# A hybrid attention trunk on one core: the next head's keys are turned two blocks earlier, the old head's end one block later

## The chip, the core and the metric

The kernel runs on one core of a Trainium2 chip. Its engines each work through an instruction stream of their own and meet at semaphores: TensorE (PE in the profile, with its weight loads as PEld), VectorE (DVE), ScalarE (ACT, called Activation below), GpSimd (POOL) and SyncE (SP), which issues most of the transfers. The metric is the device time of one execution in microseconds, lower is better. A comparison is between medians of several runs on the same chip.

## What is computed

One layer of a diffusion trunk over 512 latent tokens and 128 context tokens, width 1024, all in float32: a gated feed-forward half-step, a token mixer, a second half-step. The change lies in the mixer's differential attention, 8 heads, each with two query/key pairs of width 64 and a value of width 128:

```python
dq = rmsnorm(dq.reshape(B, T, DA_HEADS, 2, DA_HEAD_DIM), p['g_qn'][l])
dk = rmsnorm(dk.reshape(B, T, DA_HEADS, 2, DA_HEAD_DIM), p['g_kn'][l])
q_att = rope_2d(dq)                                   # latent tokens
keys = jnp.concatenate([rope_2d(dk), k_ctx], axis=1)  # 512 own, 256 cached
s = jnp.einsum('bqhcd,bkhcd->bhcqk', qi, kf) * scale
pr = jax.nn.softmax(s, axis=-1)
w = pr[:, :, 0] - lam * pr[:, :, 1]
att = jnp.einsum('bhqk,bkhv->bqhv', w, vf)
att = rmsnorm(att, p['g_sub'][l]) * (1.0 - lam_init)
```

Beside it the same input projection feeds an mLSTM branch, whose gate rows also pass through this stage of the kernel.

## The kernel before, in words

Products are made float32-accurate by splitting an operand into a high part (rounded by Activation) and the rest (a subtraction on VectorE), so that one product is three matmuls (`mm3`).

**The attention stage** is a loop over 8 heads (L2091) and, in each, over 5 blocks of 128 queries (`qi` 0 to 3 latent, 4 context). A block is: `scores` (8 matmuls into one PSUM tile, of which there is one), a minimum over it on VectorE (`mn`, L1716), `soft` (two exponentials on Activation, tiles `p`), `mix` (reciprocals and one combination on VectorE), `turn` (the mixed weights are transposed on TensorE, `ps_wT`, and copied out by Activation, `wT`; in blocks 0 to 3 six transposes, in block 4 one) and `values` (matmuls into `ps_o`, scaled into `ao` by VectorE). The steps are pipelined: `turn` and `values` of one block stand in the next.

Between these steps stand **fill units**, slices of the remaining projections (`fill.units`), which keep TensorE occupied. From head 1 on most of them are wide: 12 matmuls of 512 columns into the single tile of the pool `ps2w`, which Activation empties in two copies (`k_tok`/`q_tok`, later `v_tok`/`stage`). Other PSUM tiles of this stage rotate through four buffers (tag `mm`).

**A head's beginning.** The queries and keys lie token by token. `turned` (L1656) transposes them on TensorE (`ps_qkT`), Activation copies them to the tile `qk_t`, and four transfers lay them out as `qk_d`. `queries` then makes `qT` (one Activation copy, one VectorE subtraction), and `keys` makes `kH` and `kL` from the cached keys `ck` and from `qk_d`. Before, queries are turned in block 3 of the head ahead and keys in block 4; `queries` and `keys` stand behind that head's last block.

**A head's end.** `finish_norm` (L1757) normalises `ao` on Activation and VectorE. `finish` (L1766, kept as `late` until the next head) transposes the result (`ps_aT`), copies it to `aT` and sends that to `aT_dram`.

**One buffer for four tiles.** The tag `asq` has a single buffer, shared by `qk_t`, the square in `finish_norm`, `aT`, and in heads 2 and 4 the gate rows `QQ`, which `gate_load` (L1505) fetches at the end of block 1 and `gate_cols` (L1508) transposes on TensorE in block 2 (`ps_c`):

```python
Q_at[0] = j, load(ap, [128, T], qq_dram[:, j, :], tag="asq", name="QQ")
```

So each of these users waits until the one before has left the buffer; for `aT` that is when its transfer to `aT_dram` has landed.

**What sets the order.** TensorE's instructions keep the program's order (`mm` and `tr` call `keep_in_program_order`). Activation and VectorE instructions inside `with written():` keep the written order among themselves on their engine; the rest, and the transfers without a fixed order, are placed by the framework's scheduler when the kernel is built. On each engine and on SP's queue what comes out is a fixed sequence: an instruction that waits holds up all behind it.

**Rotations.** `rotate` (L1581) does one step at a time of the norm and rope of the next pair of heads' queries and keys, in place, on Activation and VectorE. Keys and queries of a pair of heads must be through before they are turned; in both versions they are.

Of the kernel before, what the change touches and what calls it, by code (L numbers as in the profile page):

```python
# [31 lines left out]
def tile_trunk(ctx: ExitStack, tc: tile.TileContext, a: dict):  # L32
# [35 lines left out]
    @contextmanager  # L68
    def written():
        was, as_written[0] = as_written[0], in_row  # L70
        yield
        as_written[0] = was
# [1336 lines left out]
    fill = Fill()  # L1409
# [171 lines left out]
    def rotate():  # L1581

        if not rotations:
            return False
        first, second = rotations[0], rotations[1] if len(rotations) > 1 else []
        had, left = len(first), len(second)
        with written():
            if had == 4 and left == 7 or had == 2 and left == 5:
                second.pop(0)()
            else:  # L1590
                first.pop(0)()
                if (had, left) in ((5, 8), (4, 6)):
                    second.pop(0)()
            if not first:
                rotations.pop(0)
        return True
# [190 lines left out]
    def begin_pools():  # L1787
        gates.close()
        late_p.append(late_of.enter_context(tc.tile_pool(name="late", bufs=1, reuse_waits="tile")))
        fill.spare = late_p[0]  # L1790
# [3 lines left out]
    def begin_memory():  # L1794
        assert not rotations and not any(isinstance(g[0], tuple) for g in fill.q)
        fill.spare = None
        late_of.close()
        in_pools["k"] = ctx.enter_context(tc.tile_pool(name="mlk", bufs=1, side="right", reuse_waits="tile"))
        load_keys(0)
        load_queries(0)  # L1800
# [171 lines left out]
    heads = [Head(hd) for hd in range(8)]  # L1972
# [81 lines left out]
    rope_p[0] = ap  # L2054
    gt = gates.enter_context(tc.tile_pool(name="gates", bufs=1))
    heads[0].load_cache()
    heads[0].turn_queries()
    heads[0].turn_keys()
    fill.units(3)
    heads[0].queries()  # L2060
    heads[0].keys(0, 1, 2)
    fill.units(4)
# [7 lines left out]
    def aside(hd, qi, part):  # L2070
        if hd == 0:
            for _ in range(ROWS.get((qi, part), 0)):
                next(rows, None)
        if part == 0:
            with written():
                split = fill.low()
            if qi < 4 and (UNITS[hd][qi][1] or not split):
                rotate()
        elif qi != 3:
            rotate()  # L2080
        if (qi, part) == (1, 1) and hd in (2, 4):
            gate_load(hd // 2 - 1)
        if (qi, part) == (2, 0) and hd in (2, 4):
            gate_cols()
# [5 lines left out]
    late = None  # L2090
    for hd in range(8):  # L2091
        H = heads[hd]
        odd = hd % 2
        N = heads[hd + 1] if hd < 7 else None
        for qi in range(5):
            n = UNITS[hd][qi]
            with written():
                H.scores(qi)
                if qi > 0:
                    H.turn(qi - 1)  # L2100
                H.soft(qi)
            aside(hd, qi, 0)
            fill.units(n[0])
            with written():
                H.mix(qi)
            if late is not None:
                late()
                late = None
            if qi > 0:
                with written():  # L2110
                    H.values(qi - 1)
            if qi == 3 and hd < 7:
                while odd and rotate():
                    pass
                with written():
                    N.turn_queries()
                N.load_cache()
            if qi == 4 and hd < 7:
                with written():
                    N.turn_keys()  # L2120
            aside(hd, qi, 1)
            if (hd, qi) == (0, 2):
                begin_pools()
            elif (hd, qi) == (6, 2):
                begin_memory()
            fill.units(n[1])
            if n[1]:
                rotate()
            with written():
                fill.ahead()  # L2130
        n = UNITS[hd][-1]
        with written():
            H.turn(4)
        if hd < 7:
            with written():
                N.queries()
                N.keys(0)
            fill.units(n[0])
            with written():
                H.values(4)  # L2140
                N.keys(1, 2)
            H.finish_norm()
            fill.units(n[1])
            with written():
                fill.ahead()
            fill.units(n[2])
            late = H.finish
        else:
            fill.eager = True
            fill.units(1)  # L2150
            H.values(4)
            H.finish_norm()
            fill.drain(3)
            with written():
                H.finish()
# [514 lines left out]
def build(nc, shapes):  # L2670
    a = {}
    for n, s in shapes.items():
        a[n] = nc.dram_tensor("in_" + n, s, F32, kind="ExternalInput").ap()
    for n, s in _OUTS.items():
        a[n] = nc.dram_tensor("out_" + n, s, F32, kind="ExternalOutput").ap()
    with tile.TileContext(nc, schedule_with_timeline_sim=True) as tc:
        tile_trunk(tc, a)
# [21 lines left out]
```

## Time and profile before

| | us |
|---|---|
| median of 3 runs | 1819.51 (1816.02 to 1820.16) |
| the profiled execution | 1823.29 |
| its span, first to last instruction | 1821.5 |
| TensorE busy | 1776.0 (98 % of the span) |
| VectorE busy | 1340.9 (74 %) |
| Activation busy | 892.9 (49 %) |
| mean granted TensorE clock | 0.995 |

The stage of the change runs from about 655 to 1095 us of the span. In the answers shown below, a row of the timeline has the start, the busy time, engine, line, operation and tiles (out<-in), how many instructions are merged in it, and in brackets the idle time ahead of it on its engine with what ended that. Rows of an engine's waits give the total, the number and the longest. `SPq` marks SP's queue, on which the time is that of issuing a transfer; the time to its landing is told apart.

### The profile page before, as it was taken

The page shows a single profiled execution, that of the slowest core. Times are in us where ns is not written, and L with a number is a line of the kernel's source. Part 1 is how long each engine was busy: PE and PEld are TensorE (multiplying, and loading weights), DVE is VectorE, ACT ScalarE, POOL GpSimd, SP SyncE. Part 2 cuts the span into 40 slices and gives each one's busy share as a digit, 9 for nine tenths or more (in the row PEclk, how much of TensorE's full clock was granted, in tenths as well). Part 3 has the DMA queues.
Part 4 walks back from the last instruction along what each step waited for, and adds up shares of the span by engine and source line. Part 5 has one row for each costly group of instructions (what it writes and reads, how often), then busy time and mean ns, then how long its engine had stood idle before and what let it go on. Part 6 is the DMA issues. An engine that isn't in the chain of part 4 may idle for free.

```text
span 1821.5 us, 29435 instructions
## 1 busy us (share of the span) xinstructions
PE 1776.0 (98%) x11790; PEld 1706.8 (94%) x11790; DVE 1340.9 (74%) x2136; ACT 892.9 (49%) x1563; POOL 40.8 (2%) x72
## 2 busy tenths in 40 slices
PE   8999999989999999999999999999999999999998
PEld 6999999989999999877878998889999999999998
DVE  5979987667888848667675546877677888997485
ACT  4554544332655455555654536563326545454432
POOL 0000000100000000000000000000000000000010
PEclk9999999999999999999999999999999999999999
DMA  8355566968235553333334336566652445557992
GB/s 310 125 197 167 187 236 222 348 207 275 90 115 194 189 171 81 106 108 103 105 112 128 116 97 235 178 217 219 232 175 80 133 162 194 187 184 272 354 312 87
DMA packets 150075, 328.33 MB, mean 180 GB/s; under 512 B 11633, under 2 KB 107633, under 8 KB 138161
## 3 DMA queue, kind: packets, MB, share of 16 engines
q1 hardware_dynamic: 138562, 280.69, 45.7%
q0 software_dynamic: 10688, 43.13, 7.3%
q10 hardware_dynamic: 688, 2.63, 0.4%
q8 instruction: 93, 1.52, 0.4%
q14 instruction: 44, 0.36, 0.1%
HBM read 243.77 MB, written 72.15 MB: 173 GB/s over the span
## 4 chain that ended last, share of the span: by engine, by line
PE 79%; DVE 9%; DMA 7%; ACT 3%; issue 1%; SPq 1%; ACTq 0%; DVEq 0%
PE ps_f L75 48%; PE ps_p L75 14%; PE ps_t L75 7%; PE sc L75 2%; PE ps_o L75 2%; DVE ww L54 2%; DMA qk_d<-qk_t 2%; PE ps_n L75 1%; DMA raw_a<-in_w_ada_k 1%; DMA P<-nm_dram 1%; DVE wL L54 1%; PE ps_wT L78 1%; DMA raw<-in_w2a 1%; DMA raw<-in_w2b 1%; DVE mn L1716 1%
## 5 line engine op out<-in xcount | busy, mean ns | idle before, releaser
L75 PE MATMUL ps_f<-S,ww 128*128 128x320 f32 x2400 | 387.2, 309 | 2.7 <-DMA S<-g_dram 1.1
L75 PEld LDWEIGHTS ps_f<-S,ww 128*128 128x128 f32 x2400 | 359.8, 188 | 6.8 <-DVE ww L54 4.6
L54 DVE TENSOR_TENSOR ww<-raw,ww 128x2048 fp32r<-128x2048 f32 (+1 forms) x73 | 163.9, 2246 | 65.9 <-ACT ww L51 65.8
L75 PE MATMUL ps_f<-hm,ww 128*128 128x320 f32 x1176 | 187.0, 311 | 4.5 <-ACT ps_f L51 4.4
L75 PEld LDWEIGHTS ps_f<-hm,ww 128*128 128x128 f32 x1176 | 177.0, 189 | 5.0 <-ACT ps_f L51 4.7
L51 ACT ACTIVATE ww<-raw 128x2048 fp32r<-128x2048 f32 (+1 forms) x73 | 136.8, 1874 | 57.9 <-DVE raw L54 39.6
L54 DVE TENSOR_TENSOR raw<-raw 128x1024 f32<-128x1024 f32 x186 | 161.2, 867 | 2.4
L75 PE MATMUL ps_f<-hm,wB 128*128 128x320 f32 x1008 | 161.5, 309 | 0.0
L75 PE MATMUL ps_t<-wH,hH 128*128 128x256 f32 (+1 forms) x440 | 153.2, 348 | 6.2 <-ACT stage L51 3.9
L75 PE MATMUL ps_p<-hH,wH 128*128 128x320 f32 x480 | 150.9, 314 | 1.4 <-DVE num L54 1.4
L75 PEld LDWEIGHTS ps_f<-hm,wB 128*128 128x128 f32 x1008 | 151.3, 188 | 0.0
L75 PE MATMUL ps_t<-wH,hL 128*128 128x256 f32 (+1 forms) x440 | 148.2, 337 | 0.9 <-DVE hL L54 0.9
L75 PE MATMUL ps_p<-hH,wL 128*128 128x320 f32 x480 | 148.3, 309 | 0.0
L75 PE MATMUL ps_p<-hL,wH 128*128 128x320 f32 x480 | 148.3, 309 | 0.0
L75 PE MATMUL ps_t<-wL,hH 128*128 128x256 f32 (+1 forms) x440 | 148.1, 337 | 0.0
L51 ACT ACTIVATE u<-ps_f 128x320 f32<-128x320 f32 x129 | 55.8, 433 | 155.6 <-PE ps_f L75 155.5
L54 DVE TENSOR_TENSOR wL<-raw,wH 128x2048 fp32r<-128x2048 f32 x37 | 84.7, 2288 | 25.4 <-ACT wH L51 24.2
L54 DVE TENSOR_TENSOR wB<-raw,wB 128x1024 fp32r<-128x1024 f32 x64 | 78.2, 1221 | 31.3 <-ACT wB L51 31.3
L75 PEld LDWEIGHTS ps_t<-wH,hH 128*128 128x128 f32 x440 | 85.5, 194 | 15.4 <-ACT stage L51 5.1
L51 ACT ACTIVATE wH<-raw 128x2048 fp32r<-128x2048 f32 (+1 forms) x45 | 75.3, 1679 | 48.3 <-PE ps_p L75 38.6
L814 DVE CUSTOM_DVE_ANT_0 junk<-raw_a,csil 128x1024 bf16<-128x1024 f32 (+1 forms) x76 | 92.7, 1219 | 3.2 <-DMA raw_a<-in_w_ada_c 3.0
L75 PEld LDWEIGHTS ps_t<-wH,hL 128*128 128x128 f32 x440 | 85.5, 194 | 9.9 <-DVE hL L54 1.1
(304 smaller groups left out, 3538.2 us busy)
## 6 DMA issues: line engine op xcount, KB each, us to landing
g_dram<-g SPq DMA_DIRECT2D x44, 640.0 KB, 7.5
raw_a<-in_w_ada_c POOLq DMA_DIRECT2D x38, 512.0 KB, 5.2
g_dram<-g SPq DMA_DIRECT2D x24, 480.0 KB, 8.2
raw<-in_w1b SPq DMA_DIRECT2D x11, 1024.0 KB, 4.9
raw<-in_w3b SPq DMA_DIRECT2D x11, 1024.0 KB, 6.3
raw<-in_w1a SPq DMA_DIRECT2D x10, 1024.0 KB, 5.0
raw<-in_w3a SPq DMA_DIRECT2D x10, 1024.0 KB, 6.2
qk_d<-qk_t SPq DMA_DIRECT2D x64, 160.0 KB, 2.9
```

The source lines that it names most:

```text
L51: return placed(nc.scalar.activation(*args, **kw))
L54: return placed(eng.tensor_tensor(out=out, in0=in0, in1=in1, op=op))
L75: tc.keep_in_program_order(nc.tensor.matmul(*args, **kw))
L78: tc.keep_in_program_order(nc.tensor.transpose(*args, **kw))
L814: placed(vec.tensor_tensor_reduce(out=junk, in0=raw, in1=self.csil[:, v, :], op0=ALU.mult, op1=ALU.add, scale=1.0, scalar=0.0, accum_out=m ...
L1716: placed(vec.tensor_reduce(out=mn, in_=sv, axis=AX.X, op=ALU.min))
```

## The change

Four things move; no instruction is added or removed.

1. The next head's keys are turned in block 2 (before: block 4) and its queries in block 3, as before. The kernel's first head turns its keys first too, with one fill unit between keys and queries.
2. `finish` of the old head (`late`) runs in block 1 of the new head, between the fill unit and `values(0)` (before: in block 0), and its order is now a written one.
3. At a head's end `queries` of the next head stands ahead of the transposes of the last block (`turn(4)`).
4. The line that flushed pending rotations in block 3 of odd heads is gone.

```diff
     heads[0].load_cache()
+    heads[0].turn_keys()
+    fill.units(1)
     heads[0].turn_queries()
-    heads[0].turn_keys()
-    fill.units(3)
+    fill.units(2)
     heads[0].queries()
     heads[0].keys(0, 1, 2)
...
             with written():
                 H.mix(qi)
-            if late is not None:
-                late()
+            if late is not None and qi == 1:
+                with written():
+                    late()
                 late = None
             if qi > 0:
                 with written():
                     H.values(qi - 1)
+            if qi in (2, 3) and hd < 7:
+                with written():
+                    (N.turn_keys, N.turn_queries)[qi - 2]()
             if qi == 3 and hd < 7:
-                while odd and rotate():
-                    pass
-                with written():
-                    N.turn_queries()
                 N.load_cache()
-            if qi == 4 and hd < 7:
-                with written():
-                    N.turn_keys()
             aside(hd, qi, 1)
...
         n = UNITS[hd][-1]
-        with written():
-            H.turn(4)
         if hd < 7:
             with written():
                 N.queries()
+                H.turn(4)
                 N.keys(0)
...
         else:
+            with written():
+                H.turn(4)
             fill.eager = True
```

How the sequences move is shown at three places. The first is **SP's queue in blocks 0 to 2 of head 2**, where `raw` are fill weights from HBM (512 KB each), `stage` an emptied fill unit, and `aT_dram`, `QQ` and `qk_d` the transfers named above. Before:

```order
L97 DMA raw<-in_w_dk 128x4x256
L97 DMA raw<-in_w_dq 128x4x256
L1773 DMA aT_dram<-aT 128x640
L1830 DMA v_dram<-stage 128x256
L97 DMA QQ<-qq_dram 128x640
L97 DMA raw<-in_w_dv 128x4x256
L97 DMA raw<-in_w_mv 128x4x256
L1830 DMA v_dram<-stage 128x256 x2
L1668 DMA qk_d<-qk_t 64x640 x8
```

and with the change:

```order
L97 DMA raw<-in_w_dk 128x4x256
L97 DMA raw<-in_w_dq 128x4x256
L1830 DMA v_dram<-stage 128x256
L97 DMA raw<-in_w_dv 128x4x256
L97 DMA raw<-in_w_mv 128x4x256
L1773 DMA aT_dram<-aT 128x640
L97 DMA QQ<-qq_dram 128x640
L1830 DMA v_dram<-stage 128x256
L1668 DMA qk_d<-qk_t 64x640 x4
```

`aT_dram` and `QQ` moved behind the two weight loads, and `QQ` now stands directly behind `aT_dram`, whose buffer it takes over. Head 4 has the same picture with one load of 1024 KB (`raw<-in_w_mq`) in place of the two.

The second place is **TensorE in the same head, from the end of block 1's fill unit into block 2**, with the change:

```order
L78 MATMUL ps_aT<-ident,ao 128x128 x5
L75 MATMUL ps_o<-v_tok,wT 128x128 x6
L75 MATMUL sc<-kH,qT 128x512
L75 MATMUL sc<-kL,qT 128x512
...
L78 MATMUL ps_wT<-ident,p_8130 128x128 x6
L78 MATMUL ps_c<-ident,QQ 128x128 x5
L75 MATMUL ps_t<-wH,hH 128x512
```

Before, the first row stood a fill unit, the scores and the transposes of block 1 further ahead; all the others are where they were. Between the transposes of the finished head (`ps_aT`) and those of the gate rows (`ps_c`) there are now only `values(0)`, the scores of block 2 and one `turn`.

The third place is **Activation at the end of head 2**, from the exponentials of block 4 (`p`, 128x128) to the square of `finish_norm`:

```order
 L51 ACTIVATE wT<-ps_wT 128x256
-L51 ACTIVATE p_8365,sm<-sc,mn 128x128
-L51 ACTIVATE p_8366,sm<-sc,mn 128x128
-L51 ACTIVATE qk_t<-ps_qkT 128x512
-L51 ACTIVATE qk_t<-ps_qkT 128x128
+L51 ACTIVATE p_8380,sm<-sc,mn 128x128
+L51 ACTIVATE p_8381,sm<-sc,mn 128x128
+L51 ACTIVATE qT<-qk_d 128x1280
 L51 ACTIVATE wT<-ps_wT 128x128
-L51 ACTIVATE qT<-qk_d 128x1280
 L51 ACTIVATE kH<-ck 128x2x256
-L51 ACTIVATE v_tok<-ps_t 128x256
-L51 ACTIVATE stage<-ps_t 128x256
 L51 ACTIVATE kH<-qk_d 128x2x512
 L51 ACTIVATE kH<-qk_d 128x2x128
+L51 ACTIVATE v_tok<-ps_t 128x256
+L51 ACTIVATE stage<-ps_t 128x256
 L51 ACTIVATE asq<-ao 128x640
```

The copies of the turned keys are gone from here (they are in block 2), `qT` stands ahead of the last turned weights, and the two copies that empty the fill unit (`v_tok`, `stage`) stand behind both `kH` copies from `qk_d` instead of ahead of them.

## The prediction

> **What bounds the kernel now.** I read the page's busy shares first, then TensorE's own waits in the attention stage, then the timeline around the largest of them.
>
> ```profile
> PE 1776.0 (98%) x11790; PEld 1706.8 (94%) x11790; DVE 1340.9 (74%) x2136; ACT 892.9 (49%) x1563; POOL 40.8 (2%) x72
> ```
>
> TensorE is the bound: the change can move the end only by what TensorE waits for, or by its clock. Its waits between 655 and 1095 us (total, times, longest):
>
> ```profile
> PE ps_aT L78 <- DVE ao L54: 8.4, 5, 2.6
> PE ps_t L75 <- ACT stage L51: 3.9, 5, 1.2
> PE ps_o L75 <- ACT wT L51: 2.9, 2, 2.4
> PE sc L75 <- ACT p L51: 1.8, 1, 1.8
> PE ps_t L75 <- ACT q_tok L51: 1.1, 2, 0.5
> ```
>
> The largest is the transposing of the old head's result, which comes before VectorE has normalised it. Its instances in heads 1 to 5, by the timeline:
>
> ```profile
> 751.59 0.66 PE L78 MATMUL ps_aT<-ident,ao 128*128 128x128 f32 x4 [1.18 <-DVE ao L54]
> 797.40 0.76 PE L78 MATMUL ps_aT<-ident,ao 128*128 128x128 f32 x5 [1.08 <-DVE ao L54]
> 846.63 0.77 PE L78 MATMUL ps_aT<-ident,ao 128*128 128x128 f32 x5 [2.48 <-DVE ao L54]
> 892.54 0.76 PE L78 MATMUL ps_aT<-ident,ao 128*128 128x128 f32 x5 [1.04 <-DVE ao L54]
> 941.83 0.77 PE L78 MATMUL ps_aT<-ident,ao 128*128 128x128 f32 x5 [2.62 <-DVE ao L54]
> ```
>
> **Term 1: the old head's end, one block later.** There `ao` is ready long before: in head 3 it is done when the transposes start, 846.6, and the new place lies behind another fill unit and the scores. So the wait goes, and nothing of the work: heads 1, 3 and 5 give 1.18 + 2.48 + 2.62 = 6.3 us. Heads 2 and 4 are counted in term 2, by absolute times.
>
> **Term 2: the gate rows in heads 2 and 4.** `QQ` takes the buffer that `aT` leaves, and `ps_c` waits for `QQ` in TensorE's fixed order. SP's queue before, and TensorE at the consumer and at the next wait, for head 2 (around 800) and head 4 (around 900):
>
> ```profile
> 800.14 0.34 SPq L1773 DMA_DIRECT2D aT_dram<-aT  x1
> 802.31 0.32 SPq L97 DMA_DIRECT2D QQ<-qq_dram  x1
> 806.37 0.38 SPq L97 DMA_DIRECT2D raw<-in_w_dv  x1
> 806.81 0.50 SPq L97 DMA_DIRECT2D raw<-in_w_mv  x1
> 901.48 0.33 SPq L97 DMA_DIRECT2D raw<-in_w_mq  x1
> ...
> 808.97 0.71 PE L78 MATMUL ps_c<-ident,QQ 128*128 128x128 f32 x5
> 815.00 0.50 PE L75 MATMUL ps_t<-wH,hH 128*128 128x512 f32 x1 [1.18 <-ACT stage L51]
> 904.14 0.71 PE L78 MATMUL ps_c<-ident,QQ 128*128 128x128 f32 x5
> 910.12 0.50 PE L75 MATMUL ps_t<-wH,hH 128*128 128x512 f32 x1 [1.18 <-ACT stage L51]
> ```
>
> Before, `QQ` was issued 6.7 us ahead of `ps_c` and no wait shows. With the change `aT` is copied behind block 1's exponentials. Activation's rows before:
>
> ```profile
> 801.92 1.90 ACT L51 ACTIVATE wH<-raw 128x2048 fp32r<-128x2048 f32 x1
> 805.34 0.91 ACT L51 ACTIVATE p<-sc,mn 128x768 f32<-128x768 f32 x1
> 848.53 0.93 ACT L51 ACTIVATE aT<-ps_aT,gs 128x512 f32<-128x512 f32 x2
> ```
>
> The exponentials end at 806.2. TensorE runs 1.1 us earlier once its wait at 797.40 is gone, but Activation is held by the weight copy `wH`, and I take only 0.4 us of it: 805.8, plus two `aT` copies of 0.93, is 806.75; the transfer starts at 806.85. The weight loads, which VectorE releases when it has split the weights of `wH`, come about 0.5 earlier than their 806.37 and 806.81: 1 MB is issued at 805.9 and 806.3, ahead of `aT` in the same queue. The landings:
>
> ```profile
> raw<-in_w_mv SPq DMA_DIRECT2D x8, 512.0 KB, 5.2
> raw<-in_w_mq SPq DMA_DIRECT2D x3, 1024.0 KB, 4.9
> aT_dram<-aT SPq DMA_DIRECT2D x8, 320.0 KB, 2.2
> QQ<-qq_dram SPq DMA_DIRECT2D x2, 320.0 KB, 3.0
> qk_d<-qk_t SPq DMA_DIRECT2D x64, 160.0 KB, 2.9
> ...
> L1668 SPq DMA_DIRECT2D qk_d<-qk_t x4: 482/596/606, 727.8 to 729.6; - x4
> DMA to landing us min/median/max: 5.0/5.9/6.6
> ```
>
> The last two rows are key transfers issued in head 0 right behind such a pair of loads, and they need 5.0 to 6.6 us where the typical one of their kind needs 2.9. So `aT` lands between 806.85 + 2.2 = 809.1 and 806.85 + 6.6 = 813.5; I take 812.3, 0.8 behind the weights (806.3 + 5.2 = 811.5). `QQ` needs 3.0 more and 0.05 to be issued: 815.3, bounds 812.1 and 816.5. Against 808.97 that is +6.4 (3.1 to 7.6). While TensorE stands, Activation catches up, so the 1.18 us at 815.00 goes: +5.2 (1.9 to 6.4) for head 2, its own 1.08 included. TensorE itself would be there at about 808.0, so it waits some 7 us. In head 4 the load starts near 901.0 and lands at 905.9, `aT`, issued at 902.0, at 906.7, `QQ` at 909.7: +5.6 on 904.14, less 1.18 is +4.4 (bounds 902.0 + 2.2 + 3.05 = 907.25, +1.9; 902.0 + 5.3 + 3.05, +5.0). Together **+9.6** (3.8 to 11.4). Queued behind `ps_c` on TensorE is everything, so nothing hides it; behind the waiting `QQ` on SP stand only the stores and key transfers of block 2.
>
> **Term 3: the clock after such a wait.** Windows of 3.41 us in and behind a wait; the column behind POOL's is the granted clock:
>
> ```profile
> 698.21:701.62 3.41, 1.59 (x9) 1.15 (x8) 1.43 (x4) 3.41 (x6) 0.00 (x0) 1.00 0.54 87
> 701.62:705.03 3.41, 3.41 (x17) 3.38 (x17) 3.38 (x4) 2.59 (x5) 0.00 (x0) 0.50 0.22 25
> 846.70:850.10 3.40, 3.40 (x18) 2.90 (x19) 2.35 (x3) 2.76 (x4) 0.00 (x0) 1.00 0.31 108
> ```
>
> The 1.8 us wait of `sc` (among the waits above) left TensorE 1.59 of 3.41 busy, and the next 3.41 ran at half clock; after the 2.48 us at 846.63 the clock stayed at 1.00. So waits near 2 us may or may not cost a window, and one of 7 us, which fills a window and more, will: 3.41 x 0.5 = 1.7 us each, **+3.4** (0 to 5.1, half as much again if the window in which TensorE resumes is short of work too). None of the waits of term 1 that I quote a clock for paid this, so none is credited. The Trainium skill ("TensorE: Matmul & The Clock Gate", "Why this matters for your kernels") says that idle gaps over about 3 us drop the clock to half. The wait of 1.8 us is below that and paid, so the measurement decides; by the page's rule the change trades waits too short to be gated for two that are long enough, and the sum stays the same.
>
> **Term 4: the end of a head.** Head 2 before:
>
> ```profile
> 825.46 8.22 SPq L1668 DMA_DIRECT2D qk_d<-qk_t  x8
> 830.50 0.77 ACT L51 ACTIVATE qk_t<-ps_qkT 128x512 f32<-128x512 f32 x2 [3.24 <-PE ps_qkT L78]
> 831.31 1.29 ACT L51 ACTIVATE qT<-qk_d 128x1280 fp32r<-128x1280 f32 x1
> 832.48 0.64 ACT L51 ACTIVATE kH<-ck 128x512 fp32r<-128x512 f32 x1
> 833.76 0.38 ACT L51 ACTIVATE stage<-ps_t 128x256 f32<-128x256 f32 x1
> 834.19 0.50 PE L75 MATMUL ps_t<-wH,hH 128*128 128x512 f32 x1 [0.53 <-ACT stage L51]
> 836.10 1.36 ACT L51 ACTIVATE kH<-qk_d 128x1024 fp32r<-128x1024 f32 x2 [1.97 <-DMA qk_d<-qk_t]
> ```
>
> Activation's 1.97 us for the keys' transfer goes, but TensorE never waited for that. TensorE waits for `stage`, which empties the one wide PSUM tile, and `stage` now stands behind `qT`, `wT` and both `kH`. The queries' four transfers start from 825.46, 0.6 us apart, the last at 827.25; with the 2.9 above it lands at 830.15. Then `qT` 1.2, `wT` 0.2, `kH` 0.6 and 1.3, `v_tok` and `stage` 0.65: 834.1. That is the time of before, while the keys' transposes, 0.5 us of TensorE, have moved ahead of the queries' and push this chain by as much. So about +0.46 for each of the five ends with a wide unit (three waits for `stage`, two for `q_tok`, 0.53 each, in the waits above): **+2.3**. Bounds: -2.65 if all five waits vanish, +4.5 if the copies come another 0.4 later.
>
> **Term 5: head 0.** The 2.4 us wait for `wT` loses the keys' copies ahead of it (0.8) and gains the 0.5 of transposes; the first `sc` wait hangs on a chain of gate rows that stands in another order with the same work. **-0.3**, from -7 (both waits and their half-clock windows gone, 1.8 + 2.4 + 3.4 less the 0.5) to +1.
>
> Removing the flush of rotations moves nothing on the path: the rope steps keep their order on VectorE.
>
> Sum: -6.3 + 9.6 + 3.4 + 2.3 - 0.3 = **+8.7 us**. The profiled execution took 1823.29, so it would take 1832.0; that execution was 3.8 above the median of the runs, so the median goes from 1819.5 to about **1828**, +0.5 %.
>
> **The rivals.**
>
> *Short trip of the gate rows.* `aT` and `QQ` pass beside the weight loads: term 2 is at its floor of 3.8, the waits are some 4 us and pay half of the windows (1.7). -6.3 + 3.8 + 1.7 + 2.3 - 0.3 = +1.2, 1820.7. For it: typical `aT` landings of 2.2. Against it: 5.0 to 6.6 behind loads.
>
> *Head 0 opens up.* Its two waits and windows go, term 5 is -7: +2.0, 1821.5. For it: keys first, so 0.8 us of copies leave the chain; against it: the queries' transfers there still land 6.6 us late behind weights.
>
> *No wait at the gate rows (faster).* If `QQ` lands before TensorE is there, 808.0 and 903, terms 2 and 3 shrink to the two waits of 1.08 and 1.04 gained: -6.3 - 2.1 + 2.3 - 0.3 = -6.4, 1813. This decides once `aT` has landed by 805, ahead of the end of block 1's exponentials behind which its copy stands. Only another order could do that. For a gain of 0.2 % `QQ` would have to land by about 810.5 (808.97 + 1.18 + 0.35 makes terms 2 and 3 together +0.7, and the sum -3.6).
>
> **How the numbers follow.** The forecast has 0.65, the short trip 0.17, head 0 0.11, no wait 0.07. The first by itself reaches from 1823.5 (terms 2 and 3 half of the way to their floors, -4.6) to 1834 (both at their upper ends, +3.5, and half of term 4's, +2.2). The range, 1817.5 to 1834, takes in both middle cases and leaves the faster one out. About 0.2 %, 3.6 us, is what a measurement of this kernel can tell from no change: slower by more, 0.65 and a few hundredths of the middle cases, 0.70; within, most of the middle cases, 0.18; faster, 0.07 and the middle cases' low ends, 0.12.
>
> **What would show it.** Right: `ps_aT` has no wait above 0.2 us; two waits of 6 to 8 us appear at `ps_c`, released by the `QQ` transfer, with `aT_dram` landing 5 us after its issue, and a half-clock window behind each; the units at the heads' ends wait about 1 us for `stage`. Wrong: waits at `ps_c` under 4 us, or `QQ` issued ahead of the weight loads; then the time falls to the old one or below. A `ps_aT` wait that stays would make it slower yet.

## The result and the profile after the change

The changed kernel takes **1822.42 us** (median of 19 runs, 1818.47 to 1826.38), the kernel before **1818.51 us** on the same chip (19 runs, 1811.63 to 1821.36). The ratio is 1.0023, 95 % interval 1.0014 to 1.0031: slower by 0.23 %, some 4 us. A second set (below) gives 1.0030 (1.0020 to 1.0040), some 5.5 us. The forecast was slower by 8.7 us, with a range of 1817.5 to 1834: sign and range hold, the size is about twice what was measured.

TensorE's waits in the attention stage after the change, by what ended them (total, times, longest):

```profile
PE ps_c L78 <- DMA QQ<-qq_dram: 13.9, 2, 7.3
PE sc L75 <- ACT p L51: 4.5, 1, 4.5
PE ps_t L75 <- ACT stage L51: 2.9, 3, 1.0
PE ps_o L75 <- ACT wT L51: 2.4, 2, 2.0
PE ps_t L75 <- ACT q_tok L51: 2.0, 2, 1.0
PE ps_wT L78 <- DVE p L57: 1.1, 2, 0.7
```

`ps_aT`, the first row before with 8.4 us, is gone from the list; the gate rows `QQ` stand at its head. (The prediction's list for the kernel before passes over one row, a wait of 1.6 us of `ps_qkT` for `g_out`. The changed kernel has the same 1.6 us, at the `ps_t` that now stands there, so nothing hangs on it.) SP's queue ahead of them in head 2:

```profile
797.63 0.37 SPq L97 DMA_DIRECT2D raw<-in_w_dv  x1
798.05 0.50 SPq L97 DMA_DIRECT2D raw<-in_w_mv  x1
798.66 0.45 SPq L1773 DMA_DIRECT2D aT_dram<-aT  x1
804.89 0.34 SPq L97 DMA_DIRECT2D QQ<-qq_dram  x1
```

`QQ` is issued 6.2 us after `aT`, which went out behind a megabyte of weights and held the one buffer until it had landed. TensorE at the two consumers:

```profile
807.79 0.66 PE L78 MATMUL ps_c<-ident,QQ 128*128 128x128 f32 x2 [7.33 <-DMA QQ<-qq_dram]
...
906.12 0.87 PE L78 MATMUL ps_c<-ident,QQ 128*128 128x128 f32 x3 [6.60 <-DMA QQ<-qq_dram]
```

That is the mechanism and the size forecast (some 7 us each). One of the five head ends, with the wait that term 4 saw growing from 0.53:

```profile
833.26 0.50 PE L75 MATMUL ps_t<-wH,hH 128*128 128x512 f32 x1 [0.97 <-ACT stage L51]
```

The first profiles do not show a slower kernel as a whole: 1823.29 us before and 1822.42 after. But in them the kernel before is late already ahead of the attention stage, where the programs are the same. So I compare one piece in both: from the last wait of the second norm to a wait of `ps_o` in head 7, the same two instructions in each program, which holds everything that was changed up to there. A row of the windows has the piece, its length, the busy time (and number of instructions) of TensorE, its weight loads, VectorE, Activation and GpSimd, the granted clock, and the share and GB/s of the DMA engines. Before:

```profile
487.90:1069.33 581.43, 561.22 (x3662) 523.69 (x3662) 406.04 (x579) 310.51 (x596) 3.69 (x7) 0.99 0.40 124
```

After:

```profile
479.82:1068.77 588.95, 561.08 (x3662) 525.24 (x3662) 407.23 (x579) 311.96 (x596) 3.69 (x7) 0.98 0.40 123
```

The piece is 7.5 us longer, all of it idle time (20.2 to 27.9 us, length less busy time); busy time, which half-clock windows make longer, did not grow. The prediction had +5.3 of waits and +3.4 of clock.

### The profile page after: what moved, and what is told of

Its sections match the earlier page's. It is cut to its first block, busy times and chain, and to the rows that moved or that the text cites. A ratio compares the mean times of both kernels' runs of the same rounds, so it can differ in the third digit from the quotient of the medians.

```text
span 1820.6 us, 29424 instructions
## 1 busy us (share of the span) xinstructions
PE 1772.2 (97%) x11790; PEld 1706.0 (94%) x11790; DVE 1341.5 (74%) x2136; ACT 894.2 (49%) x1563; POOL 40.8 (2%) x72
## 4 chain that ended last, share of the span: by engine, by line
PE 80%; DMA 7%; DVE 7%; ACT 4%; issue 1%; SPq 1%; ACTq 0%; DVEq 0%
PE ps_f L75 49%; PE ps_p L75 14%; PE ps_t L75 7%; PE sc L75 2%; PE ps_o L75 2%; DVE ww L54 2%; DMA qk_d<-qk_t 1%; PE ps_n L75 1%; DMA P<-nm_dram 1%; DMA raw_a<-in_w_ada_k 1%; DMA raw<-in_w2b 1%; PE ps_wT L78 1%; DVE junk L814 1%; PE ps_u L75 1%; SPq L1668 1%
```

## The experiments

**1. Both kernels again, unchanged** (1818.35 us, ratio 1.0007, 0.9996 to 1.0017; and 1822.1 us, 1.0030).

> The kernel before, unchanged, for a second profile and the clock of each of its runs. In the first pair of profiles the piece from the second norm (about 480) to the end of the attention stage (about 1070) took 581.4 us before and 589.0 after, +7.5, while the medians differ by 4. Theory E (the first profile of the kernel before was untypical in a part that the change does not touch: three half-clock windows in and around head 0): this profile has at most two of them there, and the piece is 576 to 580 us. Rival F (the piece is truly 7.5 us longer after the change, and something outside of it gives back 3.5): 581 us again, and the mean clock of the runs as in the first profile, 0.995.

> The changed kernel, unchanged, for a second profile on the chip of the others: ratio 1.0023 as before. Theory E: the waits at ps_c are 7 us again, the first sc wait differs from 4.54 by an us or more though nothing differs in the program, and the piece from the second norm to the end of the attention stage is 585 to 589 us. Rival F: 589 us and 4.5 us again.

The piece in the second profile of before, and then of after:

```profile
480.70:1063.64 582.94, 561.20 (x3662) 522.66 (x3662) 405.81 (x579) 310.85 (x596) 3.69 (x7) 0.99 0.40 124
```

```profile
480.19:1066.17 585.98, 559.70 (x3662) 523.51 (x3662) 407.35 (x579) 312.37 (x596) 3.69 (x7) 0.99 0.40 123
```

Now +3.0 us: waits +4.5, busy time -1.5. Neither theory fits as stated: the piece of the kernel before is not shorter than in its first profile, and that of the changed kernel is. What varies with nothing changed is head 0 (its `sc` wait was 1.82 and 2.66 us before, 4.54 and 4.37 after) and where half-clock windows fall. The two longest `ps_aT` waits of the kernel before (2.48 and 2.62 us) kept the full clock in its first profile. In and behind the same two waits (2.46 and 2.60 us), the second profile shows:

```profile
835.22:838.63 3.41, 1.13 (x8) 1.05 (x9) 3.27 (x8) 3.41 (x6) 0.00 (x0) 1.00 0.81 249
838.63:842.04 3.41, 3.41 (x10) 2.64 (x9) 1.34 (x2) 1.71 (x3) 0.00 (x0) 0.50 0.36 141
930.80:934.21 3.41, 0.87 (x4) 0.38 (x2) 3.34 (x7) 2.56 (x5) 0.00 (x0) 1.00 0.89 311
934.21:937.62 3.41, 3.35 (x11) 2.87 (x12) 2.45 (x5) 2.89 (x4) 0.00 (x0) 0.50 0.10 37
```

Both waits paid here. So three more profiles of each kernel were taken.

> The kernel before, a third profile. Clock theory: TensorE is busy 560.5 to 561.5 us in the stage (its own half-clock windows cost it 4 to 5 us, in head 0 or behind a ps_aT wait of 2.5 us), and idle 20 to 22 us. Head 0 theory: the clock costs it under 2 us (busy under 559) and head 0's waits (sc and wT) are under 5 us.

> The changed kernel, a third profile. Clock theory: busy 559.5 to 561.5 us in the stage, no more than before, and idle 26 to 28 us. Head 0 theory: busy 3 us more than before, and head 0's waits near those of before.

The fourth and fifth pairs were expected to show the same as the third. The times were 1813.63, 1818.43 and 1818.42 us before, 1820.92, 1828.71 and 1825.51 after. By the same rows of the windows:

| profile | 1 | 2 | 3 | 4 | 5 | mean |
|---|---|---|---|---|---|---|
| before, idle | 20.2 | 21.7 | 20.2 | 23.4 | 20.4 | 21.2 |
| after, idle | 27.9 | 26.3 | 27.0 | 28.1 | 27.4 | 27.3 |
| before, busy | 561.2 | 561.2 | 558.4 | 560.9 | 564.4 | 561.2 |
| after, busy | 561.1 | 559.7 | 559.8 | 563.5 | 559.7 | 560.8 |

Three of the busy times (558.4, 564.4, 563.5) and two of the idle times (23.4 and, barely, 28.1) lie outside the expected bands, and the third profile of the kernel before by itself fits the head 0 theory. So no single pair decides; the means do, against a head 0 that makes the changed kernel busy 3 us longer: **waits +6.1 us, busy time -0.5, the piece +5.7**, which agrees with the 4 and 5.5 us of the timed runs. The waits came as forecast (+5.3); the busy time, which term 3 let grow by 3.4, did not grow.

**2. The gate rows in a buffer that is idle at that time.** `pk` holds turned queries and keys and is free from a head's beginning until block 2.

```diff
     def gate_load(j):
-        Q_at[0] = j, load(ap, [128, T], qq_dram[:, j, :], tag="asq", name="QQ")
+        t = ap.tile([128, 2, T], F32, tag="pk", name="QQ", bufs=2)[:, 0, :]
+        dma(t, qq_dram[:, j, :])
+        Q_at[0] = j, t
```

> The changed kernel with the gate rows QQ loaded into a buffer that is free at that time (tag pk) instead of the one that aT leaves; nothing else is written differently, so QQ is issued behind the key transfers of the head before, some 20 us ahead of its use. Theory A (the two waits at ps_c and their clock windows are the loss): both waits (7.33 and 6.60 us) go, two half-clock windows of 6.83 us go (3.4 us less at half speed), and the two waits for stage (1.18 each) may come back: -13.9 - 3.4 + 2.4 = -14.9 against the change, 1807.5 us, some 11 us faster than the kernel before. Rival B (the 3.9 us between the medians say that most of the two waits is made up elsewhere, since the profiles' stage is 8.5 us longer): taking them away gives back only what they cost net, about 4 to 8 us: 1814 to 1818, no more than 0.2 % under the kernel before.

**1805.64 us, ratio 0.9937 (0.992 to 0.9954)**: 15.6 us less than the change by the two ratios (1.0023 less 0.9937, of 1818), and faster than the kernel before. `QQ` is now issued at

```profile
776.27 0.34 SPq L97 DMA_DIRECT2D QQ<-qq_dram  x1
```

and `ps_c` has left the waits, of which the first rows are

```profile
PE sc L75 <- ACT p L51: 3.4, 1, 3.4
PE ps_t L75 <- ACT stage L51: 2.9, 3, 1.0
```

`aT` still goes out behind the two weight loads (796.98, the loads at 795.95 and 796.36); only `QQ` no longer stands behind it. Theory A is right: nothing makes the two waits good elsewhere. The 1.18 us waits for `stage` in block 2 did not come back; so they are not something that Activation catches up on while TensorE stands, as the prediction had it.

**3. The old head's end one block later, alone, on the kernel before**; and the same with `QQ` moved as in 2.

```diff
-            if late is not None:
-                late()
+            if late is not None and qi == 1:
+                with written():
+                    late()
                 late = None
```

> The kernel before with only one part of the change: the old head's end (ps_aT, aT) one block later, in written order; turning, queries and the first head are as before. Theory A: waits of ps_aT go (-6.3), two waits of about 7 us appear at ps_c (+9.6 net) with their half-clock windows (+3.4): +6.7, 1825 us, ratio about 1.0037, which is more than the whole change costs by its median (+3.9). Rival B: this part costs as much as the whole change or less, +2 to +4: 1820.5 to 1822.5.

> The kernel before with the old head's end one block later and QQ in a free buffer; keys, queries and the first head as before. This is term 1 of the prediction without terms 2 and 3. Theory A: the waits of ps_aT (8.4 us) go, the waits for stage of 1.18 us in block 2 stay (VectorE's order is that of before): -8.4 less the clock windows that such waits cost in some executions (up to 3): -8 to -11, ratio 0.994 to 0.9955. Rival J: what the late ao held up goes on to another wait (of sc or of ps_wT, since VectorE does the same work in the same order), half of the gain is lost: ratio 0.997 to 0.998.

Alone 1822.33 us, ratio 1.0027 (1.0015 to 1.0039), +4.9; with `QQ` moved 1808.36 us, **0.9945 (0.9926 to 0.9964)**, -10.0. The first lies between the two expectations by its ratio (its time, 1822.33, is at the top of B's), the second is theory A. Its first waits:

```profile
PE sc L75 <- ACT p L51: 4.1, 3, 3.5
PE ps_o L75 <- ACT wT L51: 2.8, 2, 2.3
PE ps_t L75 <- ACT stage L51: 1.9, 4, 0.5
```

No `ps_aT`, and no 1.18 us wait either (the longest for `stage` is 0.5). So the one-block delay does take its waits away, and sharing the buffer with `QQ` turns 10 us of gain into 5 of loss.

**4. The first head as before, the rest as changed.**

```diff
-    heads[0].turn_keys()
-    fill.units(1)
     heads[0].turn_queries()
-    fill.units(2)
+    heads[0].turn_keys()
+    fill.units(3)
     heads[0].queries()
```

> The changed kernel with the first head as before (queries, then keys, then three fill units); the rest of the change stays. Theory A: the first sc wait goes from 4.54 back to about 1.8 us and its clock loss from 6.83 us at half speed to 3.41 (1.7 us less), the waits for wT stay near 2.4 in all: -2.7 - 1.7 = -4.4 against the change, 1818.0, no different from the kernel before. Rival (the first head's order is worth nothing, its waits trade with the clock by chance): 1822.4, as the change.

1822.31 us, 1.0030 (1.0019 to 1.0041), as the change. Its `sc` wait was 2.15 us in the one profile, but that bought nothing that the runs can tell. The rival holds, and theory A misses: the head's order has no measurable price of its own.

**5. The old head's end back in block 0; and the early keys alone.** In the first, `qi == 1` of the change becomes `qi == 0`. In the second, the kernel before is changed in one place:

```diff
+            if qi == 2 and hd < 7:
+                with written():
+                    N.turn_keys()
             if qi == 3 and hd < 7:
...
-            if qi == 4 and hd < 7:
-                with written():
-                    N.turn_keys()
```

> The changed kernel with the old head's end back in block 0 (in written order), everything else as changed. Theory A: aT and QQ are issued ahead of the weight loads again, so the waits at ps_c and their windows go (-17.3) and the waits for stage come back (+2.4), while the waits of ps_aT come back, 8.4 us in all before: -6.5 against the change, 1816. Rival C (turning the keys earlier takes the keys' copies from the head's end, so VectorE and Activation finish the norm of ao earlier or later): the waits of ps_aT are then under 4 us (1811) or over 12 us (1820).

> The kernel before with only the next head's keys turned in block 2 instead of block 4; the old head's end, the queries and the first head are as before. The prediction gave this part nothing to gain and 0.46 us to lose at each of five head ends: +2.3, ratio 1.0013. Rival D (from the run with the old head's end back in block 0, 9 us faster than before): with the keys' copies gone from the head's end, VectorE's order there changes too, the normalising of ao stands ahead of the weight subtraction wL and of the minimum mn, and TensorE's waits for ao fall from 8.4 to about 3.5 us and the waits for stage in block 2 (1.18 each) go: -4.9 - 2.4 + 2.3 = -5, ratio 0.997 or, with fewer half-clock windows, 0.995.

Block 0: 1808.22 us, **0.9955 (0.9939 to 0.997)**, below what A had (1816), rival C's first case: its `ps_aT` waits are 3.5 us in all. Early keys alone: **1802.92 us, 0.9921 (0.9909 to 0.9933)**, 14.4 us faster, more than any theory here gave it. All waits of `ps_aT` are gone without the delay. In its one profile the piece has 9.5 us of idle time, against a mean of 21.2 before: 8.7 of `ps_aT` are gone, 2.5 of head 0's wait for `wT` and 2.4 of the two 1.18 us waits, while the head ends take 1.6 more and `ps_wT` 0.4. VectorE at the beginning of head 3 before, ahead of the `ps_aT` that waited 2.48 us until 846.63:

```profile
839.93 2.29 DVE L54 TENSOR_TENSOR wL<-raw,wH 128x2048 fp32r<-128x2048 f32 x1 [0.24 <-ACT wH L51]
842.14 0.16 DVE L57 SCALAR_TENSOR_TENSOR rt<-ry 128x5 f32<-128x5 f32 x1
842.22 1.75 DVE L1716 TENSOR_REDUCE mn<-sc 128x2 f32<-128x1536 f32 x1
...
845.55 0.17 DVE L57 SCALAR_TENSOR_TENSOR ry<-rt,ry 128x5 f32<-128x5 f32 x1
845.75 0.83 DVE L54 TENSOR_TENSOR ao<-ao,ry 128x640 f32<-128x640 f32 x1
```

and with the early keys:

```profile
823.66 0.17 DVE L57 SCALAR_TENSOR_TENSOR rt<-ry 128x5 f32<-128x5 f32 x1 [0.52 <-ACT ry L51]
823.87 0.17 DVE L54 TENSOR_TENSOR rt<-rt,rv 128x5 f32<-128x5 f32 x1
824.07 0.17 DVE L57 SCALAR_TENSOR_TENSOR ry<-rt,ry 128x5 f32<-128x5 f32 x1
824.27 0.82 DVE L54 TENSOR_TENSOR ao<-ao,ry 128x640 f32<-128x640 f32 x1
825.60 2.29 DVE L54 TENSOR_TENSOR wL<-raw,wH 128x2048 fp32r<-128x2048 f32 x1 [0.51 <-ACT wH L51]
```

The norm of the old head's result now stands ahead of the weight subtraction and the minimum. The schedule came out so once the keys' transfer stood two blocks earlier; why the scheduler chose it stays open. On the chip Activation no longer waits for that transfer: the square of the norm starts 0.24 us after TensorE has got past the head end's wait (820.84 against 820.60), before 3.2 us after it (837.38 against 834.19). I had no row for this.

**6. Only that order; and the early keys with the queries moved too.** The first edit stands in the kernel before, the second in the version with early keys:

```diff
                 N.keys(1, 2)
-            H.finish_norm()
+                H.finish_norm()
```

```diff
         n = UNITS[hd][-1]
-        with written():
-            H.turn(4)
+        if hd == 7:
+            with written():
+                H.turn(4)
         if hd < 7:
             with written():
                 N.queries()
+                H.turn(4)
                 N.keys(0)
```

> The kernel before with one edit that moves no key, query or head end: the norm at the head's end in written order, so that its small steps (rt, ry, ao) stand ahead of the weight copy wH on Activation and of the weight subtraction wL and the minimum mn on VectorE, as in the run with the keys turned early. Theory H (keys_early won by this order, not by the key transfer itself): in head 3 ao would be ready near 841.6 where TensorE stands at 844.15, so the waits of ps_aT (8.4 us) go and with them the half-clock windows that two or three of them cost (about 3 us): -8 to -11, ratio 0.994 to 0.9955. Rival I (the keys' late transfer itself is what made ao late, through the copies ahead of the square): the waits of ps_aT shrink by less than half, ratio over 0.998.

> The run with the keys turned early (ratio 0.9921) with the queries in addition ahead of the last transposes of a head, as in the change. On Activation the weight copy wH then slips between rt and ry again in heads 3 and 5, and on VectorE wL and mn stand ahead of ao there. Theory H: two waits of ps_aT of about 1.8 us come back in these heads, +3.5 and up to 1.7 of clock: ratio 0.994 to 0.995. Rival: the queries' place costs or gains nothing, 0.992.

The order alone: 1813.07 us, 0.9978 (0.9967 to 0.9989), -4.0: between the two. `ps_aT` is gone, and new waits have come. First rows of its waits:

```profile
PE ps_t L75 <- ACT stage L51: 6.4, 7, 1.3
PE ps_t L75 <- ACT q_tok L51: 4.0, 5, 1.2
```

Activation in its head 3:

```profile
827.75 1.37 ACT L51 ACTIVATE kH<-qk_d 128x1024 fp32r<-128x1024 f32 x2 [1.95 <-DMA qk_d<-qk_t]
829.02 0.72 ACT L51 ACTIVATE asq<-ao 128x640 f32<-128x640 f32 x1
831.37 0.21 ACT L51 ACTIVATE rt<-rv 128x5 f32<-128x5 f32 x1 [1.63 <-DVE rv L63]
831.61 0.21 ACT L51 ACTIVATE ry<-rt 128x5 f32<-128x5 f32 x1
831.73 1.90 ACT L51 ACTIVATE wH<-raw 128x2048 fp32r<-128x2048 f32 x1
```

With the keys still late, the norm's steps hold up the weight copy, and behind it the copies that empty the next unit. So both are needed, the early data and the order. In the version of 5 the early data brought the order with it; the next run shows that it does not in every arrangement.

The early keys with the queries ahead of `turn(4)`: 1806.96 us, 0.994 (0.9924 to 0.9956), as expected. In head 3 `wL` (828.84) and the minimum (831.13) stand ahead of `ao` (834.66) again, though the keys are early. Two of the old waits are back, one each in heads 3 and 5:

```profile
PE ps_aT L78 <- DVE ao L54: 3.5, 2, 1.8
```

**7. The emptying copies first at a head's end**, on the version of 2, and on early keys (there with the norm and the old head's end in written order too).

```diff
                 N.keys(0)
-            fill.units(n[0])
+                fill.units(n[0])
```

> The changed kernel with QQ in a free buffer, and in addition the head end's fill unit in the written order, so that its two evacuation copies stand ahead of the kH copies from qk_d again. Theory A (term 4): the five waits at the head ends go from about 1.0 back to 0.53 us each: -2.3 against the run with QQ alone (1805.6, ratio 0.9937), so ratio 0.9925 of the kernel before. Rival G: the kH copies are late instead, and the next head's first scores wait by as much: no difference, or a loss of up to 2 us.

> The run with the keys turned early, with the copies that empty the head end's fill unit ahead of the kH copies from qk_d, and the norm and the old head's end in written order so that VectorE's order stays as in that run. Theory: the five waits at the head ends go from about 0.85 to 0.53 us, -1.6 against that run: 1801.3, ratio 0.991. Rival: the kH copies come late for the next scores, no difference, 0.992.

1803.76 us, 0.9925 (0.9914 to 0.9937), exactly the ratio that term 4 gave, though the intervals of this and of version 2 overlap; the wait itself is plain. On version 2 with this edit, the same wait that the change had at 0.97:

```profile
822.57 0.50 PE L75 MATMUL ps_t<-wH,hH 128*128 128x512 f32 x1 [0.53 <-ACT stage L51]
```

On early keys: 1802.26 us, 0.9925 (0.9901 to 0.9948). Neither can be told from early keys alone (0.9921). The version to keep is therefore **the early keys alone**, one moved call.

## Why the prediction was half right

- **Term 1 (-6.3) held** for the waits. No `ps_aT` waits after; in the second pair it was 6.6 us (1.55, 2.46 and 2.60). Beside the idle time such a wait costs some overlap, which the term left out (below).
- **Term 2 (+9.6) held**: 13.9 us of waits at `ps_c`, less 1.08, 1.04 and twice 1.18, is 9.4; run 2 gives them back. Only its reason for the 1.18 was wrong.
- **Term 4 (+2.3) held**: the five waits are 2.9 + 2.0 = 4.9 us against 2.65, and go back when the order does.
- **Term 5 (-0.3)** was too low in the profiles: in the mean of five `sc` waits 4.3 us instead of 2.4, the group of `wT` 2.3 instead of 3.0, and a new wait of `ps_wT` takes 0.4, so +1.6. Run 4 found nothing of it in the time.
- **Term 3 (+3.4) is the step that failed**, where it gave the clock behind the `ps_aT` waits no credit. "None of the waits of term 1 that I quote a clock for paid this, so none is credited" took one execution for the rule. In the five profiles the piece of the kernel before lost a mean of 5.0 us to the clock (1.7 to 8.4), the changed one 6.8 (5.7 to 9.8; the busy time that falls into half-clock windows, halved): net +1.9, not +3.4. Behind the two gate rows the change lost 4.2 (3.0 to 5.7; rows of the first profile below), more than forecast. But behind the `ps_aT` waits the kernel before lost 3.4, 1.5 and 3.3 us in three of the five executions and nothing in two, a mean of 1.65. The other 0.65 is head 0, whose half-clock windows come and go in both kernels.
- **A term that the sum did not have (-2.3).** The same TensorE rows, at full clock, take that much less after the change; the prediction held them constant. Some 1.1 us of it belongs to the `ps_aT` waits. A matmul is busy 0.39 us, but where TensorE goes on, the next one starts 0.23 us after it; where TensorE waits, this overlap of 0.16 is lost beside the idle time (five times, and 0.3 in heads 6 and 7). In head 3 before, ahead of the wait that ended at 846.63, and after:

```profile
843.76 0.39 PE L75 MATMUL ps_t<-wH,hL 128*128 128x512 f32 x1
```

```profile
850.34 0.39 PE L75 MATMUL ps_t<-wH,hL 128*128 128x512 f32 x1
850.57 0.71 PE L78 MATMUL ps_aT<-ident,ao 128*128 128x128 f32 x5
```

Another 0.9 lies in the transposes of keys and queries (8.55 us of `ps_qkT` before, 7.68 after); the rest was not settled. So the sum's 8.7 becomes the measured piece: 1.5 less by term 3, 2.3 less by this, 0.8 more of waits, 5.7. The timed runs gave 4 us (2.5 to 5.6 by the interval) and 5.5 (3.6 to 7.3); how much of what separates them from 5.7 is noise stays open.

Profile of the change, the windows behind the two gate rows:

```profile
803.67:810.50 6.83, 2.71 (x9) 2.46 (x10) 2.96 (x7) 1.50 (x4) 0.00 (x0) 0.50 0.23 66
902.66:909.49 6.83, 3.37 (x11) 2.91 (x12) 2.80 (x7) 1.56 (x4) 0.00 (x0) 0.50 0.17 48
```

- **The base.** All terms were read from the first profile of before. At 1823.29 it was above all 19 runs taken beside the change, so the sum rested on one execution's clock and waits. And the upper end of the range has a slip: +2.2 is all of what term 4 had above its forecast, not half; half would make it 1832.6.
- **A step that was wrong without changing the sum**: "Activation's 1.97 us for the keys' transfer goes, but TensorE never waited for that." By the rows of run 5 it did, through the square, VectorE's order and `ao`; the profile names only the last releaser. By run 6 neither link alone gives the whole: the order without the early keys gave 4.0 us, the early keys with the old order back in two heads 10.9 of the 14.4. In the change the delay takes the same waits, so the gain was counted once. But by this step the best part of the change, worth 14 us by itself, was priced at nothing, and its parts do not add: early keys -14.4, the delay +4.9, all together +4 to +5.5.

## What to carry to other kernels

When a step is moved later, list who shares its buffer: a transfer that holds the only buffer in a queue behind weight loads is a wait on the critical engine, and a second buffer that is idle at that time may be had for nothing. Follow a wait back past its last releaser, through the orders of the engines, before saying that an earlier wait on another engine costs nothing; a part that removes a wait may make the next part unnecessary, so price the parts one by one. And compare one piece between the same instructions over several profiles: here waits repeat within a few us, and the clock alone moves the same program by up to 6 (busy time of 558.4 to 564.4 us before).

## What the hardware showed

The half-clock windows are 3.41 us long and lie on a fixed grid: in each profile their starts are whole multiples of 3.413 us apart. In the 20 profiles of these runs (20 to 1790 us of the span, counted in the trace) 60 grid windows left TensorE busy for less than 1.5 us, and each of them was followed by one at half clock; of 130 with 1.7 to 2.4 us busy, 4 were; of 21 in between, 12. In the first profile of before the 2.48 us wait lay across two grid windows, the larger part of it in the first of these (the window from 846.70 that the prediction shows begins in the middle of one):

```profile
844.98:848.39 3.41, 1.76 (x10) 1.55 (x11) 3.27 (x9) 3.41 (x5) 0.00 (x0) 1.00 0.71 239
848.39:851.80 3.41, 3.41 (x20) 2.91 (x19) 0.92 (x2) 1.73 (x5) 0.00 (x0) 1.00 0.28 111
```

and cost nothing; in the second profile a 2.46 us wait lay in one (1.13 us busy, above) and cost a window. So the rows follow the busy time in a grid window, and not the length of the wait alone. The Trainium skill ("TensorE: Matmul & The Clock Gate", "Why this matters for your kernels") puts the drop at idle gaps over about 3 us; here waits of 2.46 and 2.60 us paid it, and the measurement decides.
